# Expert results brought to their tokens by one-hot products instead of indexed stores, in a three-block network on one core

## The chip, the cores and the metric

One core of a Trainium2 chip runs the whole network in one program. The metric is the device time of that program in microseconds (us). Instructions run on TensorE (PE; its weight loads are shown as PEld), VectorE (DVE), ScalarE (ACT), GpSimd (POOL) and SyncE (SP). SP issues most transfers, POOL issues the indexed ones; 16 DMA engines move the data.

## The reference, cut to what matters

Two blocks of attention and dense layers come first and are not touched. The end of the network is a mixture of experts (T = 512 tokens of width 1024, 32 experts with a hidden width of 512, two experts for each token), then a root-mean-square norm:

```python
exp_logits = (t @ w_expert + b_expert)...            # the group is chosen first, then
top_vals, top_idx = lax.top_k(sel_logits, TOP_K)     # TOP_K = 2 experts of it
weights = jax.nn.softmax(top_vals, axis=-1) * g_w
...
hb = jax.nn.silu(xb @ w_gate[e]) * (xb @ w_up[e])    # one expert's rows
ys = hb @ w_down[e]
out = jnp.zeros((n_tok + 1, d), t.dtype).at[row_tok].add(ys * row_w[:, None])
...
x = x + out
return _rms_norm(x, g_final)
```

All is float32. One expert's weights are 6 MiB, all 32 make 192 MiB, and each is read once.

## The kernel before

`moe` runs last. The router's logits give each token its two experts; small matmuls with one-hot matrices then build, for each expert, a list of up to CAP = 64 rows: the token of each row (`li[:, 0]`), the place of its result (`li[:, 1]`, which is 2 * token + choice) and the token's norm factor. The tokens' vectors lie in device memory in `x_d`, written by `router_chunk`.

For each expert e the loop does the following.

- `gather` (L1489, POOL): an indexed transfer brings the expert's rows from `x_d` into `xg` (two buffers).
- `front` (L1495 on): ACT scales the rows (L1497), PE transposes them (L1500) into the PSUM tile `PU`, DVE applies the gain and makes `ex`; then 16 matmuls (L1510) of 64 rows by 512 columns, four for each of four weight slots, gate and up side by side in one PSUM tile (`mm` or `fmm` in turn). ACT takes the silu (L1512), DVE the product `eh`.
- `back` (L1517 on): PE transposes `eh` (L1522), DVE copies it to `ehT` (L1524), 8 matmuls with two weight slots (L1531) fill the PSUM tile `S`, ACT copies it to `ey` (L1534), and POOL stores the 64 rows by an indexed transfer into `y_d` in device memory (L1535).

`front` of expert e stands ahead of `back` of expert e - 1. The weights pass through a ring of `CAPS["ring"]` = 20 slots of 1 MiB (`slot`, L1473 on). SP issues one transfer for each slot (L1485), six for an expert, 192 in all; a slot that is used again waits for the matmuls that read it. The first use of a slot waits for a point in the program before (`gate` in `slot`): slots 0 to 4 the earliest, slots 16 to 19 the finished lists (`ready`). Tiles, waits and the order on each engine come from a scheduling layer.

After the last expert the tokens' vectors are loaded again from `x_d` (L1562), the results from `y_d` (L1607); PE adds one half of each row by matmuls with diagonal matrices of the routing weights (L1609), DVE the other half (L1610); then come squares (L1611, L1612), root, and the scaled result (L1616, L1617), stored by SP (L1618).

Between the loop and this last part stands a branch, `tc.If(most > CAP)` (L1580). Its body repeats experts with more than 64 rows. In the profiled execution the body isn't entered. Each engine loads the count into a register (L1579) and branches; on the way round the body each engine adds to its semaphores what the body would have added, after a wait for all that it has outstanding (the L1580 semaphore instructions of the trace).

Of the kernel before, what the change touches and what calls it, by code (L numbers as in the profile page):

```python
# [18 lines left out]
CAPS = dict(rT=2, m0=6, sb=1, nl=512, g0=5, w=3, wh=2, wl=2, tmp=6, lf=2, kk=2, qq=2, A=2, eu=3, kf=2, xc=2, rq=4, KH=4, KL=4, T=8, Pc=2,  # L19
            P=2, P2=2, pth=3, ptl=3, st=8, stc=2, r4=2, rsx=3, rsy=3, rst=3, hr=2, xtok=2, mh=8, ml=8,  # L20
            hh=22, hl=22, gt=10, sq=2, fw=2, fwh=2, fwl=2, yh=8, yl=8, mgh=8, mgl=8, MKH=4, MKL=4, yt=4, xt=4, ring=20, xgs=2, esg=2, eh=2, ex=2, ehT=2, ey=3, fs=4, fo=4)
# [209 lines left out]
class Net:  # L231
# [1060 lines left out]
    def router_start(self):  # L1292
        self.acc = self.tile([128, 512], F32, name="acc")
        self.pr = self.mmT("tok")
        self.x_d = self.tc.dram_tile([T, D], F32, name="x_d")

    def router_chunk(self, k):
# [8 lines left out]
        if k % 4 == 3:  # L1306

            s = slice(k // 4 * 512, k // 4 * 512 + 512)
            for b in range(4):
# [3 lines left out]
                xt = self.tile([128, 512], F32, name="xt")  # L1313
# [3 lines left out]
    def moe(self, out):  # L1317
        nc, tc = self.nc, self.tc

        list_d = tc.dram_tile([T * NE, 3], I32, name="list_d")  # L1320
        y_d = tc.dram_tile([2 * T, D], F32, name="y_d")
# [124 lines left out]
        place, entry = part(keep, 8, dt=I32), part(keep, 2, 4, 3, dt=I32)  # L1446

        def places():
            exp = part(once, 8)
            nc.gpsimd.tensor_copy(exp[:CAP, :1], last[0][:, :1])  # L1450
            pick(self.c("iota32")[:, None, None, :].to_broadcast(two), exp)
            nc.vector.scalar_tensor_tensor(place, rank, float(NE), exp, op0=OP.mult, op1=OP.add)
            nc.gpsimd.tensor_copy(entry[:, :, :, 0], self.c("tokid")[:, None, :].to_broadcast([128, 2, 4]))
            nc.gpsimd.tensor_copy(entry[:, :, :, 1], row)
            nc.gpsimd.tensor_copy(entry[:, :, :, 2].bitcast(F32), rt[:, None, :].to_broadcast([128, 2, 4]))

        def full_list():
            big = self.tmp()[:, :T * NE * 3 // 128].bitcast(I32)
# [24 lines left out]
        def weights(ap):  # L1483
            w = slot()
            nc.sync.dma_start(w, ap)  # L1485
            return w
# [8 lines left out]
        def front(xg, li_e, wgu, pool="mm"):  # L1495
# [8 lines left out]
            for t in range(4):  # L1504
                w = weights(wgu[t])
# [11 lines left out]
        def back(h, li_e, wd):  # L1517
# [8 lines left out]
            for k in range(4):  # L1526
                if k % 2 == 0:
                    w = weights(wd[k // 2])
# [11 lines left out]
        def wviews(e):  # L1540
            return [self.a[n][e] for n in ("egu", "ed")]

        lists = [[li[:CAP, 0, e:e + 1], li[:CAP, 1, e:e + 1], rtp[:CAP, e:e + 1]] for e in range(NE)]
        gather(xgs[0], lists[0])
        for e in range(NE):
            if e + 1 < NE:
                gather(xgs[(e + 1) % len(xgs)], lists[e + 1])
            w = wviews(e)
            sg = front(xgs[e % len(xgs)], lists[e], w[0], ("mm", "fmm")[e % 2])
            if e:  # L1550
                back(*last)
            last = sg, lists[e], w[1]
            if e == 0:
                places()
        y = back(*last)

        def halves(w):
            return w[:, :D], w[:, D:]
# [4 lines left out]
        dg, gf = halves(slot())  # L1563
        for i in range(8):
            nc.gpsimd.tensor_scalar(dg[:, i * 128:i * 128 + 128], self.c("ident"), s4[:, i // 2, 6 + i % 2:7 + i % 2], None, op0=OP.mult)
        idn = self.tile([128, 128], F32, name="idn")
        self.gate(idn, y)
        nc.gpsimd.tensor_copy(idn, self.c("ident"))
# [11 lines left out]
        with tc.If(most > CAP):  # L1580
            full_list()
            with tc.For_i(CAP * NE, T * NE, CAP * NE) as r0:
                with tc.For_i(0, NE, 1) as e:
                    here = nc.values_load(cnti[0:1, bass.ds(e, 1)], min_val=0, max_val=T)
                    with tc.If(here * NE > r0):
                        li2 = self.tile([CAP, 3], I32, name="li2")
                        lv = list_d[bass.ds(r0 + e, (CAP - 1) * NE + 1), :]
                        src = bass.AP(tensor=lv.tensor, offset=lv.offset, ap=[[NE * 3, CAP], [1, 3]])
                        nc.gpsimd.dma_start(li2, src)
                        lists = [li2[:, 0:1], li2[:, 1:2], li2[:, 2:3].bitcast(F32)]  # L1590
                        gather(xgs[0], lists)
                        w = [self.a[n][bass.ds(e, 1)].rearrange("a k p f -> (a k) p f") for n in ("egu", "ed")]
                        back(front(xgs[0], lists, w[0]), lists, w[1])


        nl = CAPS["nl"]
        lo, hi = slice(0, nl), slice(nl, D)
        pss = [self.mmT(("mm", "fmm", "S", "lev")[b])[:, :nl] for b in range(4)]
        for b in range(4):
            nc.tensor.matmul(pss[b], idn, xt[b][:, lo], start=True, stop=False)  # L1600
        for b in range(4):
            ps, x = pss[b], xt[b]
            yt = self.tile([128, 2, D], F32, name="yt")
            fs = self.tile([128, 4], F32, name="fs")
            o = self.tile([128, D], F32, name="fo")
            y2 = y_d[256 * b:256 * b + 256, :].rearrange("(p j) d -> p j d", j=2)
# [94 lines left out]
```

## Time and profile before

| | us |
|---|---|
| median of 3 runs | 2533.65 (2531.95 to 2535.61) |
| the profiled execution, its own time | 2530.34 |
| its span, first to last instruction | 2528.7 |
| busy in the span: PE / DVE / ACT / POOL | 2378.2 / 1354.2 / 970.2 / 118.5 |

The span is 1.6 us shorter than the execution's own time, and that is 3.3 us under the median. The page counts an engine as busy while an instruction is in it; matmuls overlap in its records (a "mean" of 394 ns doesn't mean one every 394 ns). The expert loop is the last fifth of the span: the first gather starts at 2009 us.

### The profile page before, as it was taken

Reading aid. Unit: us, or ns where it says so; the run is one execution under the profiler, and the core shown is the slowest. Engines: PE = TensorE matmul, PEld = TensorE weight load, DVE = VectorE, ACT = ScalarE, POOL = GpSimd, SP = SyncE. Lnnn points to the kernel's source line nnn. Section 1 sums busy time; section 2 is a strip of 40 time slices with the busy share of each in tenths; the row PEclk is TensorE's granted clock in tenths of the full one; section 3 lists DMA queues with packets and bytes.
Section 4 is the critical chain, followed back from the end, with each engine's and each line's share of the span. In section 5 each row is a group of like instructions: output and inputs, shape, how many; then the busy total and the mean of one; then the engine's idle time right before and its main releaser. Section 6 shows DMA issues by size and latency. Waiting matters only on the chain. (4 is left out here: it accounts for less than half of the span.)

```text
span 2528.7 us, 30232 instructions
## 1 busy us (share of the span) xinstructions
PE 2378.2 (94%) x11330; PEld 1659.3 (66%) x11331; DVE 1354.2 (54%) x3080; ACT 970.2 (38%) x1610; POOL 118.5 (5%) x179
## 2 busy tenths in 40 slices
PE   8999999999999999999999999999999798788775
PEld 6877558888888977558888887777787443222221
DVE  6788876444336878866444338867766411111112
ACT  6544554323225444554232226645444322111111
POOL 0000000000000000000000000000001111111110
PEclk9999999999999999999999999999999899999999
DMA  6133003333334132002333333132234699999997
GB/s 208 36 91 101 18 1 89 94 100 93 100 92 125 36 107 86 9 17 84 94 99 100 92 100 105 51 96 84 78 104 189 232 405 399 406 402 404 409 416 293
DMA packets 83879, 382.08 MB, mean 151 GB/s; under 512 B 12672, under 2 KB 13072, under 8 KB 58512
## 3 DMA queue, kind: packets, MB, share of 16 engines
q1 hardware_dynamic: 77744, 369.60, 41.2%
q0 software_dynamic: 5120, 8.40, 1.0%
q10 hardware_dynamic: 864, 2.10, 0.3%
q8 instruction: 90, 1.47, 0.3%
q14 instruction: 61, 0.50, 0.1%
HBM read 370.61 MB, written 12.59 MB: 152 GB/s over the span
## 5 line engine op out<-in xcount | busy, mean ns | idle before, releaser
L259 ACT ACTIVATE wh<-w 128x1024 fp32r<-128x1024 f32 (+1 forms) x264 | 276.6, 1048 | 624.0 <-PE mm L284 332.7
L283 PE MATMUL mm<-xh,wh 128*128 128x512 f32 x1232 | 489.3, 397 | 9.7 <-ACT wh L259 9.7
L284 PE MATMUL mm<-xl,wh 128*128 128x512 f32 x1232 | 485.4, 394 | 0.0
L285 PE MATMUL mm<-xh,wl 128*128 128x512 f32 x1232 | 484.3, 393 | 0.3 <-DVE wl L260 0.3
L260 DVE TENSOR_TENSOR wl<-w,wh 128x1024 fp32r<-128x1024 f32 (+1 forms) x264 | 321.0, 1216 | 173.1 <-ACT wh L259 172.0
L283 PEld LDWEIGHTS mm<-xh,wh 128*128 128x128 f32 x1232 | 232.5, 189 | 58.8 <-ACT wh L259 9.8
L284 PEld LDWEIGHTS mm<-xl,wh 128*128 128x128 f32 x1232 | 232.3, 189 | 48.7 <-issue 2.9
L285 PEld LDWEIGHTS mm<-xh,wl 128*128 128x128 f32 x1232 | 232.2, 188 | 47.8 <-DVE wl L260 0.9
L253 DVE TENSOR_TENSOR tmp<-mm,xrstd 128x512 f32<-128x512 f32 x104 | 71.7, 690 | 236.5 <-PE mm L285 230.1
L1510 PE MATMUL mm<-ring,ex 128*64 128x512 f32 x512 | 126.2, 628 | 29.5 <-DMA ring<-in_egu_dram 29.1
L1510 PE MATMUL fmm<-ring,ex 128*64 128x512 f32 x512 | 123.3, 615 | 31.5 <-DMA ring<-in_egu_dram 30.7
L283 PE MATMUL mm<-hh,wh 128*128 128x512 f32 x352 | 138.8, 394 | 0.0
L284 PE MATMUL mm<-hl,wh 128*128 128x512 f32 x352 | 138.6, 394 | 0.0
L285 PE MATMUL mm<-hh,wl 128*128 128x512 f32 x352 | 138.1, 392 | 0.0
L1531 PE MATMUL S<-ring,ehT 128*64 128x512 f32 x512 | 124.0, 608 | 11.9 <-DMA ring<-in_ed_dram 10.6
L1510 PEld LDWEIGHTS mm<-ring,ex 128*64 128x64 f32 x512 | 36.2, 142 | 118.6 <-issue 62.6
L1510 PEld LDWEIGHTS fmm<-ring,ex 128*64 128x64 f32 x512 | 35.3, 139 | 116.3 <-issue 59.6
L1497 ACT ACTIVATE xg<-xg,const 64x1024 f32<-64x1024 f32 x32 | 36.6, 1147 | 181.4 <-DMA xg<-x_d,const 181.4
L253 DVE TENSOR_TENSOR eh<-fmm,esg 64x512 f32<-64x512 f32 x16 | 11.1, 693 | 162.9 <-ACT esg L1512 162.9
L550 ACT ACTIVATE P<-S,st,const 128x128 f32<-128x128 f32 (+3 forms) x128 | 78.5, 616 | 50.3 <-DVE st L253 44.4
L253 DVE TENSOR_TENSOR eh<-mm,esg 64x512 f32<-64x512 f32 x16 | 11.1, 693 | 150.0 <-ACT esg L1512 149.9
L623 PE MATMUL O<-pth,nvh 128*64 128x512 f32 (+3 forms) x256 | 89.4, 451 | 1.0 <-DVE pth L593 0.9
(496 smaller groups left out, 4108.1 us busy)
## 6 DMA issues: line engine op xcount, KB each, us to landing
ring<-in_egu_dram SPq DMA_DIRECT2D x128, 1024.0 KB, 21.5
ring<-in_ed_dram SPq DMA_DIRECT2D x64, 1024.0 KB, 21.7
w<-in_fi_dram SPq DMA_DIRECT2D x88, 512.0 KB, 3.6
w<-in_w_dram SPq DMA_DIRECT2D x48, 512.0 KB, 3.7
w<-in_fo_dram SPq DMA_DIRECT2D x44, 512.0 KB, 3.6
w<-in_c_dram SPq DMA_DIRECT2D x16, 512.0 KB, 3.8
tmp<-tmp SPq DMA_DIRECT2D x80, 64.0 KB, 2.0
fw<-in_wo_dram SPq DMA_DIRECT2D x8, 512.0 KB, 3.5
```

Of the source, the lines that this page charges most:

```text
L253: (eng or self.nc.vector).tensor_tensor(out, a, b, op=op)
L259: nc.scalar.activation(hi, src, AF.Copy)
L260: nc.vector.tensor_tensor(lo, src, hi.bitcast(F32), op=OP.subtract)
L283: nc.tensor.matmul(ps, ah, bh, start=first, stop=False)
L284: nc.tensor.matmul(ps, ah, bl, start=False, stop=False)
L285: nc.tensor.matmul(ps, al, bh, start=False, stop=last)
L550: nc.scalar.activation(Ps[q0 + i], S[:, :n], AF.Exp, bias=b, scale=1.0 if scale is None else scale[q0 + i], accum_out=st[:, 1, i:i + 1])
L623: self.nc.tensor.matmul(out, v, p[0], start=first, stop=last)
L1497: nc.scalar.activation(xg[:CAP], xg[:CAP], AF.Copy, scale=li_e[2])
L1510: nc.tensor.matmul(ps[r], x[:, k, :], w[:, at:at + 512], start=k == 0, stop=k == 7)
L1531: nc.tensor.matmul(py[r], hT[:, k, :], w[:, at:at + 512], start=k == 0, stop=k == 3)
```

## The change

The results of two experts are kept in SBUF as a pair of tiles of 128 rows (`eyh`, `eyl`: the routing weight is applied, and the value is split into a float32r part and the rest). For each pair, DVE builds a matrix `esel` (128 rows by 512 tokens) that is 1 where a row belongs to a token (`select`); for each of 4 token blocks and 2 halves of the width PE multiplies it with `eyh` and `eyl` into the PSUM tile `X` (`to_tokens`), and DVE adds `X` to the tokens' vectors, which stay in SBUF (`xt`). `y_d` is gone from the usual path, and so is the second load of `x_d`. `places` prepares what `select` and the weights need (`crow`, `wtp`, `target`). The ring has 18 slots. The branch stands ahead of the last two experts, 30 and 31; their sum to tokens is done after it, straight into the final norm.

```diff
-CAPS = dict(..., nl=512, ..., yt=4, xt=4, ring=20, xgs=2, esg=2, eh=2, ex=2, ehT=2, ey=3, ...)
+CAPS = dict(..., ring=18, xgs=2, esg=1, eh=1, ex=2, ehT=1, eyh=1, eyl=1, esel=1, ...)
...
         def places():
...
+            nc.vector.tensor_scalar(inside, rank, float(CAP), None, op0=OP.is_lt)
+            nc.vector.scalar_tensor_tensor(code, exp, float(CAP), rank, op0=OP.mult, op1=OP.add)
+            nc.vector.scalar_tensor_tensor(code, code, 1.0, inside, op0=OP.add, op1=OP.mult)
...
+            for j in range(2):
+                pb = self.mmT("X")
+                self.spread_pe(pb, code[:, 4 * j:4 * j + 4], 4)
+                nc.scalar.activation(crow[:, j], pb, AF.Copy)
+
+            entw = self.tile([128, 8, 32], F32, name="entw")
+            for j in range(2):
+                self.tt(entw[:, 4 * j:4 * j + 4], ohs[:, 4 * j:4 * j + 4], bc(col(6 + j), 32), OP.mult)
+            pw = self.mmT("X")
+            for r in (slice(0, CAP), slice(CAP, 2 * CAP)):
+                for b in range(8):
+                    nc.tensor.matmul(pw[r, :32], hot[:, b, :], entw[:, b, :], start=b == 0, stop=b == 7)
+            nc.vector.tensor_copy(wtp, pw[:, :32])
...
-            y = self.tile([CAP, D], F32, name="ey")
-            for i, r in enumerate((one, two_)):
-                nc.scalar.activation(y[:, i * 512:i * 512 + 512], py[r], AF.Copy)
-            nc.gpsimd.indirect_dma_start(
-                out=y_d[:, :], out_offset=bass.IndirectOffsetOnAxis(ap=li_e[1], axis=0),
-                in_=y, in_offset=None, bounds_check=2 * T - 1, oob_is_err=False)
-            return y
+            return py
+
+        def weighted(py, e, ys):
+
+            r = (one, two_)[e % 2]
+            for i, s in enumerate((one, two_)):
+                yh, yl = [y[r, i * 512:i * 512 + 512] for y in ys]
+                nc.scalar.activation(yh, py[s], AF.Copy, scale=wtp[s, e:e + 1])
+                nc.vector.scalar_tensor_tensor(yl, py[s], wtp[s, e:e + 1], yh.bitcast(F32), op0=OP.mult, op1=OP.subtract)
+
+        def select(q):
+
+            sel = self.tile([128, T], F32R, name="esel")
+            nc.vector.tensor_scalar(sel, crow[:, 0], target[:, q:q + 1], None, op0=OP.is_equal)
+            nc.vector.scalar_tensor_tensor(sel, crow[:, 1], target[:, q:q + 1], sel.bitcast(F32), op0=OP.is_equal, op1=OP.add)
+            return sel
+
+        def to_tokens(ps, sel, ys, b, s, first=True):
+
+            for i, y in enumerate(ys):
+                nc.tensor.matmul(ps, sel[:, b * 128:b * 128 + 128], y[:, s], start=first and i == 0, stop=i == 1)
...
+        def finish(e, h, wd):
+
+            nonlocal ys
+            if e % 2 == 0:
+                ys = pair()
+            weighted(back(h, wd), e, ys)
+            if e % 2 and e < NE - 1:
+                sel = select(e // 2)
+                for b in range(4):
+                    for s in (lo, hi):
+                        ps = self.mmT("X")
+                        to_tokens(ps, sel, ys, b, s)
+                        self.tt(xt[b][:, s], xt[b][:, s], ps, OP.add)
...
-        for e in range(NE):
-            if e + 1 < NE:
+        for e in range(NE - 2):
+            if e + 1 < NE - 2:
                 gather(xgs[(e + 1) % len(xgs)], lists[e + 1])
...
-        xt = [v for _ in range(2) for v in halves(slot())]
-        for b in range(4):
-            nc.sync.dma_start(xt[b], self.x_d[b * 128:b * 128 + 128, :])
...
+        for e in (NE - 2, NE - 1):
+            wgu[e] = iter(list(wgu[e]))
+            if e == NE - 1:
+                wd[e - 1] = iter(list(wd[e - 1]))
+        wd[e] = iter(list(wd[e]))
...
         with tc.If(most > CAP):
...
-            nc.tensor.matmul(pss[b], idn, xt[b][:, lo], start=True, stop=False)
+            nc.tensor.matmul(pss[b], self.c("ident"), xt[b][:, lo], start=True, stop=False)
+        hs = [up(e) for e in (NE - 2, NE - 1)]
+        sel = select(NE // 2 - 1)
+        for e, h in zip((NE - 2, NE - 1), hs):
+            finish(e, h, wd[e])
+
         for b in range(4):
             ps, x = pss[b], xt[b]
...
-            nc.sync.dma_start(yt, y2)
-            for j in range(2):
-                nc.tensor.matmul(ps, dg[:, (2 * b + j) * 128:(2 * b + j) * 128 + 128], yt[:, j, lo], start=False, stop=j == 1)
-                nc.vector.scalar_tensor_tensor(x[:, hi], yt[:, j, hi], s4[:, b, 6 + j:7 + j], x[:, hi], op0=OP.mult, op1=OP.add)
+            ph = self.mmT("X")
+            to_tokens(ph, sel, ys, b, hi)
+            to_tokens(ps, sel, ys, b, lo, False)
+            self.tt(x[:, hi], x[:, hi], ph, OP.add)
```

Three places show how the order on the engines moves. The first is PE in the loop, from the results of one expert to the first slots of the expert after the next; `ring_...` are weight slots. Before:

```order
L1522 MATMUL PU<-const,eh 128x64 x4
L1500 MATMUL PU<-const,xg_15883 128x64 x8
L1531 MATMUL S<-ring_16631,ehT 64x512 x4
L1531 MATMUL S<-ring_16638,ehT 64x512 x4
L1510 MATMUL fmm<-ring_16667,ex 64x512 x4
L1510 MATMUL fmm<-ring_16674,ex 64x512 x4
```

The same place in the changed kernel:

```order
L1546 MATMUL PU<-const,eh 128x64 x4
L1524 MATMUL PU<-const,xg_15883 128x64 x8
L1555 MATMUL S<-ring_16673,ehT 64x512 x4
L1555 MATMUL S<-ring_16680,ehT 64x512 x4
L1534 MATMUL fmm<-ring_16742,ex 64x512 x3
L1576 MATMUL X<-eyh,esel 128x512
L1534 MATMUL fmm<-ring_16742,ex 64x512
L1534 MATMUL fmm<-ring_16749,ex 64x512
L1576 MATMUL X<-eyl,esel 128x512
L1534 MATMUL fmm<-ring_16749,ex 64x512 x2
L1576 MATMUL X<-eyh,esel 128x512
L1576 MATMUL X<-eyl,esel 128x512
```

The 16 products of a pair of experts now stand among the matmuls of the next `front`, three of which come between the results in `S` and the first product.

The second place is SP's queue where the weights end. Before, the last six weight transfers, the second load of the tokens and the final gain stand ahead of the branch:

```order
L1485 DMA ring_16536<-in_egu_dram 128x2048
L1485 DMA ring_16555<-in_ed_dram 128x2048
L1485 DMA ring_16598<-in_ed_dram 128x2048
L1562 DMA ring_16612<-x_d 128x1024
L1570 DMA ring_16631<-in_g_final_dram 128x1024
L1579 TENSOR_LOAD cmaxi
L1580 COMPARE_AND_BRANCH
```

In the changed kernel, with the branch's two ends and what follows it (the rows of the body, which isn't entered, lie between the two fences):

```order
L1509 DMA ring_16680<-in_ed_dram 128x2048
L1509 DMA ring_16742<-in_ed_dram 128x2048
L1509 DMA ring_16749<-in_ed_dram 128x2048
L1509 DMA ring_16456<-in_egu_dram 128x2048
L1509 DMA ring_16477<-in_egu_dram 128x2048
L1632 TENSOR_LOAD cmaxi
L1633 COMPARE_AND_BRANCH
```

```order
L1633 UNCONDITIONAL_BRANCH x2
L1509 DMA ring_16557<-in_egu_dram 128x2048
L1509 DMA ring_16578<-in_egu_dram 128x2048
L1509 DMA ring_16599<-in_ed_dram 128x2048
L1509 DMA ring_16640<-in_ed_dram 128x2048
L1623 DMA ring_16647<-in_g_final_dram 128x1024
L1694 DMA out_dram<-fo 128x1024 x4
```

Of the 192 weight transfers 184 stand ahead of the branch (the last four of them are expert 30's gate and up), and 8 stand behind it: expert 31's gate and up, and both experts' down weights.

The third place is PE around the branch. Before, two of the four products that bring the tokens into PSUM stand ahead of it and two behind, and no expert's matmul is behind it. In the changed kernel this comes behind it:

```order
L1673 MATMUL tok<-xt_16154,const 128x512
L1524 MATMUL PU<-const,xg_15881 128x64 x8
L1524 MATMUL PU<-const,xg_15883 128x64 x8
L1534 MATMUL mm<-ring_16456,ex 64x512 x4
L1534 MATMUL fmm<-ring_16578,ex 64x512 x4
L1546 MATMUL PU<-const,eh 128x64 x4
L1555 MATMUL S<-ring_16606,ehT 64x512 x4
L1555 MATMUL S<-ring_16640,ehT 64x512 x4
L1576 MATMUL tok<-eyh,esel 128x512 x4
```

All 48 matmuls of experts 30 and 31 stand behind the branch (a row or two of each kind are shown), after four products of the tokens' vectors with the identity.

## Rows read from the trace of the kernel before

**Rows 1.** The page, GB/s moved in 40 equal slices of the span (63 us each).

```profile
GB/s 208 36 91 101 18 1 89 94 100 93 100 92 125 36 107 86 9 17 84 94 99 100 92 100 105 51 96 84 78 104 189 232 405 399 406 402 404 409 416 293
```

**Rows 2.** SP queue's waits, 1900 to 2529 us: total us, times, longest us.

```profile
SPq L1485 <- DMA ring<-in_egu_dram: 249.6, 104, 3.8
```

**Rows 3.** Timeline of POOL: start us, us; first and last gather (15 apart), two stores (3 apart).

```profile
2180.76 0.94 POOL L1489 DMA_INDIRECT xg<-x_d,const  x1 [11.86 <-PE PU L1500]
...
2428.57 0.94 POOL L1489 DMA_INDIRECT xg<-x_d,const  x1 [11.88 <-PE PU L1500]
...
2447.64 0.92 POOL L1535 DMA_INDIRECT y_d<-ey,const  x1 [15.03 <-ACT ey L1534]
...
2492.84 0.89 POOL L1535 DMA_INDIRECT y_d<-ey,const  x1 [14.30 <-ACT ey L1534]
```

**Rows 4.** Two windows: length, busy by engine, PE's granted clock, DMA share, GB/s.

```profile
1936.00:1946.00 10.00, 9.50 (x39) 7.80 (x40) 5.09 (x17) 2.25 (x3) 3.33 (x15) 0.83 1.01 422
...
2505.00:2507.00 2.00, 1.72 (x2) 0.84 (x3) 0.00 (x0) 0.00 (x0) 0.00 (x0) 0.50 0.42 74
```

**Rows 5.** DMA queues, 2433 to 2494 us: POOL's queue: packets, MB, share.

```profile
q0 software_dynamic: 380, 0.55, 2.5%
```

**Rows 6.** Timeline of PE, 2049 to 2125 us, one expert that waits for nothing.

```profile
2049.49 7.06 PE L1510 MATMUL fmm<-ring,ex 128*64 128x512 f32 x32
2056.49 0.46 PE L1522 MATMUL PU<-const,eh 64*128 64x64 f32 x4
...
2057.51 3.65 PE L1531 MATMUL S<-ring,ehT 128*64 128x512 f32 x16
2060.97 7.07 PE L1510 MATMUL mm<-ring,ex 128*64 128x512 f32 x32
```

**Rows 7.** Timeline of PE at 1900 us: two of a run of float32r products.

```profile
1900.22 0.39 PE L283 MATMUL mm<-mgh,wh 128*128 128x512 f32 x1
...
1900.45 0.39 PE L284 MATMUL mm<-mgl,wh 128*128 128x512 f32 x1
```

**Rows 8.** Groups of DVE, 2505 to 2529 us: busy us, mean ns, idle before.

```profile
L1610 DVE SCALAR_TENSOR_TENSOR ring<-yt,const,ring 128x512 f32<-128x512 f32 x8 | 6.0, 751 | 20.3 <-DMA yt<-y_d 20.3
```

**Rows 9.** Timeline of SP at the loop's start: weight transfers issued.

```profile
2011.79 2.15 SPq L1485 DMA_DIRECT2D ring<-in_egu_dram  x4
2020.04 2.19 SPq L1485 DMA_DIRECT2D ring<-in_ed_dram  x2
```

**Rows 10.** DMA issues: KB of one, median us from issue to landing.

```profile
memt<-in_memT_dram SPq DMA_DIRECT2D x1, 1024.0 KB, 4.8
```

**Rows 11.** Timeline of all engines, 2465 to 2529 us.

```profile
2474.17 0.20 PEld L1531 LDWEIGHTS S<-ring,ehT 128*64 128x64 f32 x4 [0.20 <-DMA ring<-in_ed_dram]
...
2494.25 0.20 PEld L1531 LDWEIGHTS S<-ring,ehT 128*64 128x64 f32 x4 [1.31 <-DMA ring<-in_ed_dram]
...
2505.28 2.04 PE L1600 MATMUL mm<-ring,idn 128*128 128x512 f32 x2 [5.73 <-issue]
...
2507.12 1.59 PE L1600 MATMUL S<-ring,idn 128*128 128x512 f32 x2
...
2511.58 0.63 ACT L1612 ACTIVATE fo<-ring 128x512 f32<-128x512 f32 x1 [14.08 <-DVE ring L1610]
...
2512.33 0.60 ACT L1611 ACTIVATE fo<-mm 128x512 f32<-128x512 f32 x1
...
2513.03 1.28 ACT L1614 ACT_TABLE_LOAD   x1
...
2524.07 0.74 DVE L1617 SCALAR_TENSOR_TENSOR fo<-ring,fs,ring 128x512 f32<-128x512 f32 x1
```

**Rows 12.** Chain that ended last: start us, us, what.

```profile
2462.83 41.06 DMA y_d<-ey,const
```

**Rows 13.** Instructions of the branch's line: duration ns, first and last start us.

```profile
L1580 SPq EVENT_SEMAPHORE  x7: 17/17/17, 2488.3 to 2498.7; - x7
...
L1580 POOLq INC_SWDGE_SEM  x1: 1464/1464/1464, 2502.5 to 2502.5; - x1
```

More of the change, by code (lines that the diff above doesn't have):

```diff
@@ L1295, in router_start @@
         self.x_d = self.tc.dram_tile([T, D], F32, name="x_d")
+        self.xt = [self.tile([128, D], F32, name=f"xt{b}") for b in range(4)]
     def router_chunk(self, k):
@@ L1481, in slot, with loads @@
             return ring[i % nring]
[L1483 to L1486, printed above, removed]
+        def loads(ap, n, spare=None):
+            for t in range(n):
+                w = slot() if spare is None else spare[t % len(spare)]
+                nc.sync.dma_start(w, ap[t])
+                yield w
         def gather(xg, li_e):
@@ L1504, in front @@
             for t in range(4):
-                w = weights(wgu[t])
+                w = next(wgu)
                 for kk in range(2):
@@ L1527, in back @@
                 if k % 2 == 0:
-                    w = weights(wd[k // 2])
+                    w = next(wd)
                 for i, r in enumerate((one, two_)):
@@ L1550, in moe @@
             if e:
-                back(*last)
-            last = sg, lists[e], w[1]
+                finish(*last)
+            last = e, h, wd[e]
             if e == 0:
                 places()
-        y = back(*last)
-        def halves(w):
-            return w[:, :D], w[:, D:]
-        xt = [v for _ in range(2) for v in halves(slot())]
-        for b in range(4):
-            nc.sync.dma_start(xt[b], self.x_d[b * 128:b * 128 + 128, :])
-        dg, gf = halves(slot())
-        for i in range(8):
-            nc.gpsimd.tensor_scalar(dg[:, i * 128:i * 128 + 128], self.c("ident"), s4[:, i // 2, 6 + i % 2:7 + i % 2], None, op0=OP.mult)
@@ L1591, in moe @@
-                        gather(xgs[0], lists)
-                        w = [self.a[n][bass.ds(e, 1)].rearrange("a k p f -> (a k) p f") for n in ("egu", "ed")]
[L1593 to L1598, printed above, removed]
-        for b in range(4):
-            nc.tensor.matmul(pss[b], idn, xt[b][:, lo], start=True, stop=False)
+                        src = bass.AP(tensor=lv.tensor, offset=lv.offset, ap=[[NE * 4, CAP], [1, 4]])
@@ new lines, in moe @@
+                        for s in (one, two_):
+                            nc.gpsimd.dma_start(li2[s], src)
+                        li_e = [li2[:CAP, 0:1], li2[:CAP, 1:2], li2[:CAP, 2:3].bitcast(F32)]
+                        gather(xgs[0], li_e)
+                        w = [self.a[n][bass.ds(e, 1)].rearrange("a k p f -> (a k) p f") for n in ("egu", "ed")]
+                        h = front(xgs[0], li_e, loads(w[0], 4, spare))
+                        py = back(h, loads(w[1], 2, spare))
+                        y = self.tile([CAP, D], F32, name="ey")
@@ new lines, in moe @@
+                        for i, s in enumerate((one, two_)):
+                            nc.scalar.activation(y[:, i * 512:i * 512 + 512], py[s], AF.Copy, scale=li2[s, 3:4].bitcast(F32))
+                        nc.gpsimd.indirect_dma_start(
+                            out=y_d[:, :], out_offset=bass.IndirectOffsetOnAxis(ap=li_e[1], axis=0),
+                            in_=y, in_offset=None, bounds_check=2 * T - 1, oob_is_err=False)
+            for b in range(4):
+                y2 = y_d[256 * b:256 * b + 256, :].rearrange("(p j) d -> p j d", j=2)
+                nc.sync.dma_start(yt.rearrange("p (j d) -> p j d", j=2), y2)
+                for j in range(2):
+                    self.tt(xt[b], xt[b], yt[:, j * D:j * D + D], OP.add)
```

60 lines of the change are left out of this document (37 added, 23 removed).

## Prediction

> **What bounds the kernel now.** I read the page's slices first: from the 33rd on, the engines move 399 to 416 GB/s without a gap [rows 1], and the last fifth of the span, the experts, is bound by the weights. The waits of SP say the same: 249.6 us in 104 waits for a weight transfer to land before the next may start [rows 2]. A window in which SP's queue alone runs gives the rate, 422 GB/s [rows 4]; 6 MiB of one expert take 14.9 us at it, one transfer 2.48 us. In the timeline of POOL an expert takes 16.52 us (15 gathers in 247.8 us) where gather and store run, and 15.07 us (three stores in 45.2 us) at the end, where the gathers are over [rows 3]. PE, when it waits for nothing, needs 11.48 us for an expert, from one `front` to the next [rows 6]; it has some 5 us of slack in each. So in the loop only DMA time counts.
>
> The end is different. The last weight arrives at 2494.25 [rows 11], and the chain of waits ends in the indexed stores, which it follows for 41.06 us, one behind the other [rows 12]. After them come the loads from `y_d` and the norm, 34.5 us from the last weight to the end at 2528.7. Between them lies the branch. Its rows show what it is: SP stands from 2488.3 to 2498.7 in semaphore instructions of the branch until its transfers have landed; POOL ends its part at 2502.5 + 1.46 = 2504.0 [rows 13], and PE's first product behind it starts at 2505.28 [rows 11], 1.3 us later. It joins all engines and all transfers.
>
> **The sum.** The landmark is the landing of weight transfer 184, the last one ahead of the branch in the changed kernel. Before, its matmuls are released at 2474.17 [rows 11], and 54.5 us are left.
>
> *Two slots fewer* cost time at the loop's start. Before, slots 16 to 19 are filled by the four transfers at 2011.79; the next transfer needs the first slot back and is issued at 2020.04 [rows 9]. With 18 slots two transfers, 5.0 us of DMA time, fall out of this gap: a transfer takes 4.8 us when it is alone [rows 10], so the engines run dry until about 2023. The engines never idle later, so it isn't won back. The two products `entw` on DVE, ahead of the lists, add some tenths. Together 5.2 us; one transfer (2.5) to three (7.5) are the bounds, three because the small products of `places` also hold up PE's second expert, which frees the next slots. A gain is excluded: nothing is loaded earlier.
>
> *No stores into `y_d`*: 29 of them lie ahead of the landmark. One costs 15.07 - 14.9 = 0.2 us by the periods, and 2.5% of 61 us over four stores = 0.38 us by POOL's share of the engines [rows 5]. I take 0.3: 8.7 us off, bounds 5 and 11. The gathers stay. The second load of `x_d` stands behind the last weight in SP's queue and takes nothing from this landmark.
>
> Transfer 184 then lands at 2474.2 + 5.2 - 8.7 = 2470.7.
>
> *The products of a pair* cost PE 16 x 0.23 = 3.7 us [rows 7], DVE eight additions and two comparisons at 0.75 [rows 8]. A pair then needs 2 x 11.48 + 3.7 = 26.7 us of PE against 32.4 us of DMA: nothing, with 5.8 us of cover for waits between PE and DVE over `X`. `ey` becomes `eyh` on ACT at the same size; `eyl` adds 1.5 us of DVE per expert, off the path.
>
> *The branch* now waits for the additions of experts 28 and 29. Expert 29's down weights land four transfers, 9.9 us, ahead of transfer 184. From there: its matmuls 1.8 (half of 3.65 [rows 6]), `eyh` 0.6, `eyl` twice 1.5, a product 0.5, eight additions 6.0, the last comparisons 1.5, which DVE does ahead of the branch, 11.9 us in all, and 1.3 to release everyone: 13.2 - 9.9 = 3.3 us behind the landmark. Everything behind the branch waits for it, SP's last eight weight transfers too (for SP's own transfers, at least). Bounds: 1.3, when the additions are hidden, and 8, when products and additions alternate instead of overlapping.
>
> *Behind the branch* PE does four products with the identity, of which the trace shows one at 2.04 and a second at 1.59 [rows 11]: with two at full rate (half of 2.04) 5.7 us. Then transposes and `ex` 1.6, two times the 7.0 us of up and gate, two times 1.0 + 3.46 for the transposes and the down product [rows 6]: 30.2 us. The gathers are issued by then. The eight transfers need 4.8 + 7 x 2.48 = 22.2 us from a start at about the landmark, so each lands before PE comes to it: the bound changes from DMA to PE.
>
> [...]
>
> *The norm.* The first result in PSUM 1.9 us after the last down matmul, six squares at 0.75, the table load 1.28, root and reciprocal 0.5, eight scaled products 6.0 and small steps 0.6, then 3.9 us from the last DVE instruction (2524.07 + 0.74) to the end [rows 8, 11]: 18.7 us, bounds 17 and 22. The store and load of `y_d` that stood here are gone.
>
> End: 2470.7 + 3.3 + 30.2 + 18.7 = 2522.9 against 2528.7, 5.8 us less. The profiled execution's own time, 2530.34, becomes 2524.5; the median of the runs is 3.3 us above that execution, so I forecast 2528 us. Most of what the stores give back is lost at the ring, and the two experts behind the branch fill nearly all the time that the loads of `y_d` took.
>
> **Rivals.**
>
> The clock, *slower*: after the branch PE works at the lower level through experts 30 and 31. For: the idle stretch ahead of it is about the one that halves it in [rows 11]. Against: there it recovers within two products, and here PE has work without a gap. Price: 14.0 + 6.9 us of matmuls twice as long, 20.9 us, 2549 us. It decides from 5.8 us of matmul time at half rate on. Chance 0.11.
>
> *No change*: the ring costs its upper bound (7.5) and the additions ahead of the branch overlap only in part (6 instead of 3.3). 5.0 us more, 2533 us. For: both rest on PE waiting for DVE at places which the trace doesn't have. Chance 0.22.
>
> The stores cost what gathers cost, *much faster*: 16.52 - 15.07 = 1.45 us each, 42 us instead of 8.7, 2495 us. For: both move 64 rows of 4 KB by index. Against: 15.07 us with stores is hardly above the bare weights. Chance 0.05.
>
> PE becomes the bound in the loop, *slower*: `X` makes a pair wait over 5.8 us. At 8 us it is 2.2 x 14 = 31 us, 2559 us. Against: PE has matmuls of the next expert between the products. Chance 0.04.
>
> **How the numbers follow.** The forecast has 0.58; its own range, from the bounds added as independent, is 2521 to 2534. With the no-change case inside and half of the clock's case reached, the range is 2518 to 2540. A measurement here can tell 0.2%, 5.1 us, from no change; the forecast lies just beyond, so I give two thirds of its chance to faster, and with the gather case that is 0.45; the rest of it and nearly all of the no-change case make 0.37 for the same; the two slow rivals and the upper edge 0.18.
>
> **What would show it.** The waits of PE for weights stay in the loop, and the period is near 16.2 us. DMA share drops for some microseconds near 2018 and at the branch. Transfer 184 lands near 2471, PE's first product behind the branch starts near 2474, the last down matmul ends near 2504. It is wrong if PE waits for `X` or DVE in the loop, if matmuls behind the branch take about twice 0.43 us, or if the loop's period falls well under 16.

## The result, and the profile after

The changed kernel takes 2628.83 us, the median of four runs (2626.69 to 2633.76), against 2534.63 us (2531.95 to 2538.32) for the kernel before on the same chip: a ratio of 1.0373 (95% interval 1.0361 to 1.0386). It is 94 us slower, where 2528 us were forecast. The profiled execution took 2628.70 us, its span is 2627.1 us, 98.4 us longer than before.

Of its page, the granted clock (tenths of full speed) and the GB/s in 40 slices (66 us each):

```profile
PEclk9999999999999999999999999999998899899998
GB/s 200 42 104 81 9 17 96 97 96 97 97 120 62 62 128 25 1 73 96 96 97 96 97 109 48 93 86 88 104 200 276 355 349 318 318 347 318 321 385 53
```

The expert loop no longer moves 399 to 416 GB/s [rows 1] but 318 to 355 in the 32nd to the 38th slice, and the granted clock falls below 0.9 in two slices of the loop, the 32nd and the 35th. SP's waits (total us, times, longest us) have changed partner too:

```profile
SPq L1509 <- PE fmm L1534: 273.2, 58, 11.8
SPq L1509 <- PE S L1555: 115.9, 55, 5.7
SPq L1509 <- PE mm L1534: 79.0, 56, 7.1
```

Before, SP waited for the transfers ahead of its own [rows 2]; now it waits for PE to give a slot back. DMA has become the one that is kept waiting. Two of POOL's gathers, eight apart, which is four pairs of experts:

```profile
2317.04 0.94 POOL L1513 DMA_INDIRECT xg<-x_d,const  x1 [11.93 <-PE PU L1524]
...
2473.99 0.94 POOL L1513 DMA_INDIRECT xg<-x_d,const  x1 [11.78 <-PE PU L1524]
```

157.0 us for four pairs are 39.2 us a pair; before it was 2 x 16.52 = 33.0 [rows 3].

**Where the 98.4 us lie.** PE's first product of expert 2 and of expert 28, in the kernel before and in the changed one:

```profile
2038.02 3.20 PE L1510 MATMUL mm<-ring,ex 128*64 128x512 f32 x14
...
2430.45 1.94 PE L1510 MATMUL mm<-ring,ex 128*64 128x512 f32 x8 [0.28 <-DMA ring<-in_egu_dram]
```

```profile
2036.64 4.92 PE L1534 MATMUL mm<-ring,ex 128*64 128x512 f32 x22
...
2532.83 2.74 PE L1534 MATMUL mm<-ring,ex 128*64 128x512 f32 x12
```

Up to expert 2 the changed kernel is 1.4 us ahead. From there to expert 28 it takes 496.2 us instead of 392.4: +103.8. From expert 28 to the end it takes 94.3 instead of 98.3: -4.0. The whole loss is in the loop, where the forecast had let PE's added work vanish behind the transfers.

**What happens in a pair.** PE at 2318 us, in the middle of the loop, and ACT in the same stretch (the counts are of trace records: the 512 float32 matmuls of `front`, 512 columns wide, have 1024 of them, the 256 new float32r products 256):

```profile
2318.95 0.50 PE L1576 MATMUL X<-eyh,esel 128*128 128x512 f32 x1 [0.78 <-ACT eyh L1563]
2319.38 1.07 PE L1534 MATMUL fmm<-ring,ex 128*64 128x512 f32 x2
...
2320.81 1.08 PE L1534 MATMUL fmm<-ring,ex 128*64 128x512 f32 x4
2326.45 1.22 PE L1576 MATMUL X<-eyh,esel 128*128 128x512 f32 x2 [4.57 <-ACT eyh L1563]
...
2328.03 1.97 PE L1534 MATMUL fmm<-ring,ex 128*64 128x512 f32 x2
```

```profile
2318.21 0.68 ACT L1563 ACTIVATE eyh<-S,const 64x512 fp32r<-64x512 f32 x1 [3.83 <-PE S L1555]
2324.54 1.15 ACT L1521 ACTIVATE xg<-xg,const 64x1024 f32<-64x1024 f32 x1 [5.65 <-DMA xg<-x_d,const]
2325.72 0.68 ACT L1563 ACTIVATE eyh<-S,const 64x512 fp32r<-64x512 f32 x1
```

`eyh` is made in two halves from the same tile `S`, so both could start at 2318. The second stands behind the scaling of a later expert's rows (L1521), and that waits 5.65 us for a gather which POOL issued at 2317.04. Nothing needs those rows yet: PE transposes them at 2355.69, 31 us later. PE does what matmuls of `front` it has ahead of the product, then stands for 4.57 us. When it goes on, two records of `front` take 1.97 us, where two took 1.07 ahead of the stall. The stall and the 6 us behind it as windows (length; busy us of PE, PEld, DVE, ACT, POOL; granted clock, DMA share, GB/s), and the whole loop:

```profile
2321.00:2326.00 5.00, 0.89 (x4) 0.00 (x1) 0.60 (x1) 1.43 (x2) 0.00 (x0) 0.88 1.02 359
2326.00:2332.00 6.00, 5.55 (x8) 1.70 (x8) 2.13 (x3) 0.40 (x1) 0.00 (x0) 0.53 0.59 218
2036.00:2533.00 497.00, 424.94 (x1786) 150.55 (x1784) 168.78 (x262) 80.16 (x104) 24.32 (x26) 0.93 0.88 337
```

Behind the stall the granted clock is 0.53 over 6 us, where it was 1.00 from 2316 to 2321 us. So one wait is paid twice: once idle, once at nearly half rate (1.97 us for what took 1.07).

The order on ACT late in the loop, before and after the change, shows that the scaling (L1497, now L1521) has moved. It stood behind both halves of `ey`; now it stands between the halves of `eyh`. Why the scheduling layer put it there, the runs don't show:

```
before                                           changed
L1534 ACTIVATE ey<-S 64x512 x2                   L1536 ACTIVATE esg<-mm 64x512
L1497 ACTIVATE xg_15883<-xg_15883,const 64x1024  L1563 ACTIVATE eyh<-S,const 64x512
L1512 ACTIVATE esg<-mm 64x512                    L1521 ACTIVATE xg_15881<-xg_15881,const 64x1024
                                                 L1563 ACTIVATE eyh<-S,const 64x512
                                                 L1536 ACTIVATE esg<-fmm 64x512
```

The wait itself isn't new. ACT's wait for the gathers, in the kernel before over 2036 to 2440 us:

```profile
ACT xg L1497 <- DMA xg<-x_d,const: 155.6, 28, 9.4
```

and in the changed kernel over 2036 to 2533 us, with PE's largest wait there:

```profile
ACT xg L1521 <- DMA xg<-x_d,const: 148.3, 25, 9.1
...
PE X L1576 <- ACT eyh L1563: 59.7, 21, 5.4
```

155.6 us of waiting cost nothing before: both halves of `ey` were out by then, and only a store waited for them. Now one half stands behind that wait, and PE's products wait for it. ACT's rows above show it: the second half of `eyh` started at 2325.72 us, 0.03 us after the end of the scaling, and not at 2318.21, when the first half started from the same tile.

**The end** came out about as counted. PE behind the branch:

```profile
2578.26 6.61 PE L1673 MATMUL tok<-xt,const 128*128 128x512 f32 x8 [3.52 <-DMA xg<-x_d,const]
...
2586.45 7.09 PE L1534 MATMUL mm<-ring,ex 128*64 128x512 f32 x32 [0.43 <-DVE ex L253]
```

The products with the identity take 6.6 us (5.7 forecast), the next matmuls run at full rate, and from 2578.26 to the end of the span it is 48.8 us; 30.2 + 18.7 = 48.9 was forecast.

### The profile page after: what moved, and what is told of

It is laid out like the page before. It is cut to its first block, busy times and chain, and to the rows that moved or that the text cites. A ratio compares the mean times of both kernels' runs of the same rounds, so it can differ in the third digit from the quotient of the medians.

```text
span 2627.1 us, 30810 instructions
## 1 busy us (share of the span) xinstructions
PE 2481.3 (94%) x11606; PEld 1707.6 (65%) x11607; DVE 1496.5 (57%) x3306; ACT 976.4 (37%) x1612; POOL 89.4 (3%) x141
## 3 DMA queue, kind: packets, MB, share of 16 engines
q0 software_dynamic: 2560, 4.20, 0.5%
## 5 line engine op out<-in xcount | busy, mean ns | idle before, releaser
L1534 PE MATMUL fmm<-ring,ex 128*64 128x512 f32 x512 | 168.3, 654 | 0.8 <-DVE ex L253 0.8
L1564 DVE SCALAR_TENSOR_TENSOR eyl<-S,const,eyh 64x512 fp32r<-64x512 f32 x64 | 48.0, 750 | 205.4 <-ACT eyh L1563 205.3
L253 DVE TENSOR_TENSOR xt<-xt,X 128x512 f32<-128x512 f32 x124 | 82.0, 685 | 89.5 <-PE X L1576 89.4
L1555 PE MATMUL S<-ring,ehT 128*64 128x512 f32 x512 | 131.2, 604 | 1.4 <-DVE ehT L1548 1.2
L1576 PE MATMUL X<-eyh,esel 128*128 128x512 f32 x124 | 60.9, 508 | 61.5 <-ACT eyh L1563 61.5
L1534 PE MATMUL mm<-ring,ex 128*64 128x512 f32 x512 | 114.7, 601 | 0.7 <-DVE ex L253 0.7
L1521 ACT ACTIVATE xg<-xg,const 64x1024 f32<-64x1024 f32 x32 | 36.6, 1147 | 192.5 <-DMA xg<-x_d,const 186.8
L1576 PEld LDWEIGHTS X<-eyh,esel 128*128 128x128 f32 x124 | 25.0, 210 | 126.2 <-ACT eyh L1563 81.8
```

The lines of the kernel that those rows point to most:

```text
L253: (eng or self.nc.vector).tensor_tensor(out, a, b, op=op)
L1534: nc.tensor.matmul(ps[r], x[:, k, :], w[:, at:at + 512], start=k == 0, stop=k == 7)
L1555: nc.tensor.matmul(py[r], hT[:, k, :], w[:, at:at + 512], start=k == 0, stop=k == 3)
L1564: nc.vector.scalar_tensor_tensor(yl, py[s], wtp[s, e:e + 1], yh.bitcast(F32), op0=OP.mult, op1=OP.subtract)
L1576: nc.tensor.matmul(ps, sel[:, b * 128:b * 128 + 128], y[:, s], start=first and i == 0, stop=i == 1)
```

## Experiments

The theories, by the letters of the expectations. **S**: the scaling stands ahead of half of `eyh` in ScalarE's queue, and its wait for the gather holds up PE. **L**: ScalarE has too much work or the results come too late, whatever the order. **P**: PE's own work with the products, and its waits for `X`, are the bound. **R**: 18 slots instead of 20 starve the transfers.

**1. The scaling on another engine** (e1_scale_pool). GpSimd issues the gathers and does little else (in the loop of the changed kernel 26 instructions, 24.3 us of 497); behind a scaling only the next gather stands there.

```diff
-            nc.scalar.activation(xg[:CAP], xg[:CAP], AF.Copy, scale=li_e[2])
+            nc.gpsimd.tensor_scalar(xg[:CAP], xg[:CAP], li_e[2], None, op0=OP.mult)
```

> Only the engine that scales the gathered rows is changed (GpSimd in place of ScalarE). Theory S (ScalarE's queue: a half of eyh stands behind the scaling of rows whose gather was issued some 7 us before, TensorE waits for it, and works at the lower clock for a while after): the stall of 8.2 us per pair goes, a pair falls from 39.5 to the 32.4 us of its transfers, and the time to about 2525 us (2515 to 2540). Rival P (the sixteen products and eight additions of a pair themselves, alternating over two X tiles, are the cost): no change beyond 1%, 2605 to 2630. Rival R (the ring of 18 slots starves the transfers): no change either, 2620 to 2630.

Measured 2532.53 us beside 2533.43 of before, ratio 0.9998 (0.9986 to 1.0009). All 96 us are back with one line. The ring, the products and the single buffers of `esg`, `eh` and `ehT` (two each before) are as they were, so P and R fall as the cause of the loss, and so do the buffers. L doesn't fall by this run, since ScalarE has less to do in it. The loop as a window, the columns as above, and PE's wait there:

```profile
2040.00:2432.00 392.00, 384.06 (x1784) 140.97 (x1782) 168.24 (x262) 50.75 (x78) 99.28 (x52) 1.00 1.01 404
```

```profile
PE X L1576 <- ACT eyh L1563: 8.6, 11, 0.8
```

The scaling itself takes longer on GpSimd than the 1.15 us it took on ScalarE, which here costs nothing:

```profile
2299.34 2.84 POOL L1521 TENSOR_SCALAR xg<-xg,const 64x1024 f32<-64x1024 f32 x1 [6.75 <-DMA xg<-x_d,const]
```

The same work (1784 matmul records here, 1786 in the changed kernel) keeps PE busy for 384.1 us here and for 424.9 there, where the clock's mean is 0.93; idle is 7.9 here and 72.1 there. So the loss of 105 us between these windows is 64 us of standing and 41 us of slower work. An estimate from the pair above puts most of the 41 down to the clock: (1 - 0.53) x 6.0 = 2.8 us behind a stall, 37 us in 13 pairs.

**2. No sums in the loop** (e2_no_products). The 16 products and 8 additions of each pair in the loop are left out.

```diff
-                for b in range(4):
-                    for s in (lo, hi):
-                        ps = self.mmT("X")
-                        to_tokens(ps, sel, ys, b, s)
-                        self.tt(xt[b][:, s], xt[b][:, s], ps, OP.add)
```

> Leaves out the products to tokens and the additions of the first 15 pairs (the output lacks these experts' results); eyh, eyl, esel and the place of the scaling in ScalarE's queue stay. S and P both expect the loss to go: the loop runs at its transfers, 2510 to 2530 us. R expects 2600 or more. Between S and P the time of TensorE's up matmuls per expert tells nothing here; what it measures is the price of an indexed store into y_d: the period of an expert late in the loop is 16.2 us if a store costs 0.3 us, 15.1 if it costs as much as a gather.

Measured 2508.38, ratio 0.9903 (0.9883 to 0.9924), just under the 2510 to 2530 that S and P expected. With nobody in the loop waiting for `eyh`, DMA is the bound again (404 GB/s from 2240 to 2280 us), and the price of a store can be read. PE's waits from 2200 to 2420, and two gathers 11 experts apart:

```profile
PE mm L1534 <- DMA ring<-in_egu_dram: 18.8, 25, 2.1
PE fmm L1534 <- DMA ring<-in_egu_dram: 18.3, 26, 2.1
```

```profile
2211.39 0.94 POOL L1513 DMA_INDIRECT xg<-x_d,const  x1 [12.90 <-PE PU L1524]
...
2387.45 0.93 POOL L1513 DMA_INDIRECT xg<-x_d,const  x1 [14.66 <-PE PU L1524]
```

176.1 / 11 = 16.0 us an expert, against 16.52 with the store [rows 3]: a store costs about 0.5 us of DMA time. The single periods in this stretch run from 15.3 to 16.5 us, so the 0.3 that was forecast isn't excluded; the rival in which a store costs what a gather costs, 1.45, falls.

**3. Work to hold the clock** (e3_filler). 20 extra products ahead of the one that waits, whose values are not used.

```diff
+                        if b == 0 and s == hi:
+                            for _ in range(20):
+                                nc.tensor.matmul(ps, sel[:, :128], sel, start=True, stop=True)
```

> Twenty more products of a pair (esel with esel, into an X tile that is overwritten afterwards) are issued on TensorE ahead of the product that waits; nothing else is changed, and the wait on ScalarE stays. S with the clock as part of the loss: the filler (4.6 us at 0.23) lies in the wait, TensorE stays at the higher clock behind it and wins back about 2.8 us in each of 13 pairs: 2592 us (2580 to 2610). S with the wait alone: 2620 to 2635. P (TensorE is simply busy): 4.6 us more per pair, 2680 to 2690.

Measured 2661.05, ratio 1.0497 (1.0479 to 1.0516), which no expectation had. PE around the filler (L1598), and the window:

```profile
2329.68 0.46 PE L1546 MATMUL PU<-const,eh 64*128 64x64 f32 x4 [2.47 <-DVE eh L253]
...
2336.66 4.73 PE L1598 MATMUL X<-esel 128*128 128x512 f32 x17
```

```profile
2330.00:2345.00 15.00, 14.07 (x53) 8.16 (x53) 5.06 (x8) 2.52 (x3) 0.93 (x1) 0.77 0.87 336
```

The filler changed the order, so that in this pair the stall came elsewhere, ahead of it: PE waited for `eh`, and the filler itself met a clock of 0.77 (mean of the window). Over the loop (2036 to 2560 us) PE's waits for `eyh` fall from 59.7 to 32.5 us, those for `eh` rise from 11.1 to 15.8, and the filler adds more than is saved: 17 of its products alone take 4.73 us, some 61 us in 13 pairs. So the run doesn't tell what the clock costs; the windows of experiment 1 do.

**4. Before, with 18 slots** (e4_before_ring18). In the table of the kernel before `ring=20` becomes `ring=18`.

> The kernel before with 18 slots in its ring in place of 20, nothing else. S and the prediction's term: 5.2 us more (2.5 to 7.5), 2539 us. R: 50 us or more above the kernel before.

Measured 2533.51, ratio 0.9998 (0.9987 to 1.0009). SP at the loop's start:

```profile
2008.85 11.32 SPq L1485 DMA_DIRECT2D ring<-in_egu_dram  x4
2021.56 2.04 SPq L1485 DMA_DIRECT2D ring<-in_ed_dram  x2
```

With two slots fewer the first four transfers shown take 11.32 us to issue instead of 2.15, and the next comes at 2021.56 instead of 2020.04 [rows 9]; the time doesn't show it, and R falls a second time. The medians differ by 0.1 us, and the interval allows at most 2.3 us more, so neither the 5.2 us of the prediction nor its lower bound, 2.5, shows in the time. In the profiled execution the stretch from PE's first product of expert 0 to the end is 517.5 us against 512.4, 5.1 more, but the experts began 3.1 us earlier, and one execution of each doesn't decide it.

**5. The scaling on VectorE** (e5_scale_dve). The line of experiment 1 with `nc.vector.tensor_scalar`.

> The changed kernel with the scaling of the gathered rows on VectorE in place of ScalarE. In VectorE's order it then stands between the two halves of eyl, as it stood between the halves of eyh on ScalarE. Theory S (an engine's queue that TensorE's products need waits for a gather): the stall stays, now as a wait for eyl, 2600 to 2645 us. Rival L (ScalarE had too much to do, or is slow at it, and the place in the queue is not the cause): the time falls to that of the kernel with the scaling on GpSimd, 2525 to 2545.

Measured 2587.5, ratio 1.0202 (1.0176 to 1.0227), between the two expectations. DVE at 2300 us:

```profile
2300.00 0.74 DVE L1564 SCALAR_TENSOR_TENSOR eyl<-S,const,eyh 64x512 fp32r<-64x512 f32 x1 [1.57 <-ACT eyh L1563]
...
2305.34 0.74 DVE L1521 TENSOR_SCALAR xg<-xg,const 64x1024 f32<-64x1024 f32 x1 [4.60 <-DMA xg<-x_d,const]
2306.12 0.76 DVE L1564 SCALAR_TENSOR_TENSOR eyl<-S,const,eyh 64x512 fp32r<-64x512 f32 x1
```

ScalarE is relieved, and more than half of the loss stays: the same wait stands in DVE's queue, now ahead of the second half of `eyl`. That speaks against L. The loss is smaller than S had it: PE's waits for `eyl` sum to 34.5 us over the loop (2042 to 2496 us), where those for `eyh` in the changed kernel are 59.7. Why they are shorter was not tested.

**6. Three row buffers** (e6_xgs3): `xgs=3, ring=17`.

> The changed kernel with three buffers for gathered rows in place of two and 17 weight slots in place of 18 (to make room); the scaling stays on ScalarE, and still stands between the two halves of eyh. S: the gather is issued an expert earlier and has landed when ScalarE comes to it, ScalarE waits for no transfer, TensorE doesn't stall: 2528 to 2545 us. Rival L: no change, 2615 to 2640, since ScalarE does the same work.

Measured 2643.84, ratio 1.0426 (1.0403 to 1.045), above both expectations. S had expected the gathers to be early. They were issued an expert earlier, but the scaling moved up with them, and the wait stayed (2036 to 2533 us):

```profile
ACT xg L1521 <- DMA xg<-x_d,const: 158.0, 26, 8.7
```

My expectation missed what the order would be; the run doesn't tell S from L.

**7. The order alone** (e9_order_fix). The scaling stays on ScalarE, at the same length. Two tiny DVE instructions make its factor depend on the last column of `eyh`, times zero, so that both halves of an earlier expert's `eyh` have to stand ahead of it (for the rows of experts 3 to 29).

```diff
+        def hold(e):
+            r = (one, two_)[(e - 2) % 2]
+            z = self.tile([CAP, 2], F32, name="hold")
+            nc.vector.tensor_scalar(z[:, :1], ys[0][r, D - 1:D].bitcast(F32), 0.0, None, op0=OP.mult)
+            nc.vector.tensor_tensor(z[:, 1:2], z[:, :1], lists[e + 1][2], op=OP.add)
+            lists[e + 1][2] = z[:, 1:2]
```

> The changed kernel with the scaling left on ScalarE, two gather buffers and 18 slots; two small VectorE instructions per expert (a multiplication by zero and an addition, 64x1) write the scaling's factor only after both halves of eyh, so that on ScalarE both halves stand ahead of the scaling. Nothing else moves on TensorE. S: the loss goes, as with the scaling on GpSimd: 2532 us (2525 to 2545). L (ScalarE's load or speed is the cause): it does the same work as in the changed kernel, 2615 to 2640.

Measured 2578.21, ratio 1.0169 (1.0152 to 1.0186), about half of the loss back; S had expected 2525 to 2545, L 2615 to 2640. Its loop has two parts:

```profile
2036.00:2125.00 89.00, 88.88 (x414) 33.12 (x412) 40.78 (x72) 18.61 (x24) 5.60 (x6) 1.00 1.01 408
2125.00:2440.00 315.00, 282.53 (x1240) 98.49 (x1236) 124.58 (x221) 57.66 (x75) 16.84 (x18) 0.97 0.99 382
```

The changed kernel in the first 89 us:

```profile
2036.00:2125.00 89.00, 78.35 (x342) 28.22 (x338) 29.11 (x45) 15.17 (x20) 4.67 (x5) 0.92 0.93 356
```

There PE does 414 matmul records instead of 342 without a gap, at full clock, with ACT busier than before (18.61 against 15.17): the order is the cause, not ScalarE's load, and L falls. Later the held scaling comes so late that PE waits for it itself (2100 to 2440 us):

```profile
PE PU L1524 <- ACT xg L1521: 23.3, 8, 2.9
PE X L1576 <- ACT eyh L1563: 7.0, 9, 0.8
```

**8. The branch in the loop** (e7_branch25). With the scaling on GpSimd, the branch ahead of expert 25; all experts run in the loop, the four identity products are dropped, and the last pair goes through `X`.

```diff
-        for e in range(NE - 2):
+        for e in range(NE):
+            if e == 25:
+                finish(*last)
+                last = None
+                overflow()
```

> Scaling on GpSimd, and the branch ahead of expert 25 in place of expert 30; the last pair's sums go through X and VectorE for both halves, so the four products with the identity are gone. If the branch costs because TensorE has two experts' matmuls to do behind it (30 us) while the transfers are over: about 11 us less than with the scaling on GpSimd alone, 2517 us (2510 to 2525). If a branch costs the same wherever it stands: 2528 to 2540.

**9. The branch at the end** (e8_branch_end). The same, with `overflow()` behind all experts and sums.

> As the last, but with the branch behind all experts, where the kernel before has it. Additions of the last pair are over some 31 us after those of the pair before it began, then the branch (2.5 us), then squares, root and scaling: 2524 us (2518 to 2532). If the place ahead of the last two experts is what made the change lose its gain, this one is faster than the one with the scaling on GpSimd alone by 5 us or more; if not, it is equal or slower.

Measured 2527.25, ratio 0.9966 (0.9955 to 0.9978), and 2522.88, ratio 0.9953 (0.9935 to 0.997). The first lies between its two expectations (2510 to 2525, and 2528 to 2540), the second where it was expected. The first products of `front` of experts 24 and 28, with the branch between them (experiment 8) and without it (experiment 1):

```profile
2375.48 2.74 PE L1534 MATMUL mm<-ring,ex 128*64 128x512 f32 x12
...
2443.65 7.04 PE L1534 MATMUL mm<-ring,ex 128*64 128x512 f32 x32
```

```profile
2371.77 7.04 PE L1534 MATMUL mm<-ring,ex 128*64 128x512 f32 x32
...
2432.14 7.04 PE L1534 MATMUL mm<-ring,ex 128*64 128x512 f32 x32
```

That is 68.2 us with the branch and 60.4 without: in the loop it costs PE some 8 us. From expert 24 to expert 25 alone it is 25.6 us against 12.7, but there PE does the down products of expert 24 ahead of the branch instead of behind the next `front`. Behind all experts it costs little (experiment 12), and experiment 9 is 9.7 us faster by the medians than experiment 1, in which the last two experts stand behind the branch.

**10. The best of these** (e10_best): experiment 9, with the first two experts' rows scaled on ScalarE and the last `esel` made before the last results.

> The one with the branch behind all experts, and the first two experts' rows scaled on ScalarE (1.15 us in place of 2.84 each, at the start of the loop where TensorE waits for them); the last comparison ahead of the last additions. 3 us less than with the branch behind all experts: 2520 us (2514 to 2526).

**11. Four PSUM tiles for the pairs' products** (e11_best_lev): `self.mmT("lev")` for `self.mmT("X")`, which has two.

> As e10, with the pairs' products in four PSUM tiles in place of two X tiles. If VectorE's additions, for which TensorE's products wait with two tiles, make a pair take 30.2 us where 26.7 was counted: the loop falls back to its transfers, 2512 us (2506 to 2518). If the products, bunched further ahead, only wait for eyl instead: 2518 to 2535.

**12. No branch at all** (e12_no_branch): experiment 10 without `overflow()`, so that the repeat of overfull experts is left out.

> As e10 without the branch and its body (which this data never enters). The branch then costs what lies between the last addition and the first square, 0.7 us of it needed anyway: 2 us less than e10 (0 to 4). If the join costs more than that row shows: 5 us or more.

Measured 2519.42 (ratio 0.9938, 0.9925 to 0.995), 2516.77 (0.9921, 0.9908 to 0.9934) and 2517.75 (0.9933, 0.992 to 0.9946), beside 2535.26 of before; each lies in its expected range. Without the branch at the end it is 1.7 us less, and the intervals overlap. With four tiles a pair takes 29.1 us (2275 to 2334 us) instead of 30.2; after that it takes 30.5 to 31.6, since PE begins to wait for weights (4.3 us from 2100 to 2460 in the row below), so that its own work and the transfers are nearly level:

```profile
PE mm L1537 <- DMA ring<-in_egu_dram: 4.3, 4, 1.4
```

By the medians experiment 11 is the fastest, 0.8% under the kernel before, with the change's idea kept, its scaling on another engine and its branch moved to the end; the intervals of the three overlap.

## Why the prediction was wrong

**The step that failed** is "*The products of a pair*": "nothing, with 5.8 us of cover for waits between PE and DVE over `X`. `ey` becomes `eyh` on ACT at the same size". The size was nearly right (0.68 us a half, 1.20 for both before). What wasn't read is who waits for it and what stands ahead of it: PE now needs both halves soon after each other, and ACT's queue holds the wait for a gather between them. Half of what was needed stood in the trace of before, 155.6 us of ACT waiting for gathers; the other half stood in the order of ACT's instructions; the prediction looked at the order on PE and SP only. The clock behind a stall was considered behind the branch, not in the loop.

In the sum's own terms, a pair took PE 38.2 us (496.2 / 13) and not 26.7: 3.5 of the difference is there without the stall (30.2 in experiment 1), 4.9 is standing (64 / 13) and 3.1 slower work (41 / 13). Nothing covered the last two, 8.0 us. The cover of 5.8 us was counted against 32.4 us of transfers, but up to expert 28 the kernel before took 392.4 / 13 = 30.2 us a pair, less than its steady 33.0, since PE began with weights already in the ring.

**The rivals.** The nearest is "PE becomes the bound in the loop", with a chance of 0.04 and 2559 us. PE did become the bound, but through ACT and not through `X`. The rival let a pair wait 8 us and took 5.8 of it as covered; that a pair did lose 8.0 us is luck, since neither a queue's wait nor the clock was in it, and none of it was covered. The clock rival, a granted clock as low as the 0.50 of [rows 4] through experts 30 and 31, was placed behind the branch, where PE was back at full clock by the end of the identity products (granted 0.50 from 2578 to 2584 us, 0.95 from 2584 to 2586, 1.00 from 2586 to 2594). The clock fell in the loop (0.53 after 4.57 us idle), which the rival didn't consider, and there the wait was for an engine's queue. The rival that a store costs 1.45 us fell. (It took each list as 64 rows. The 32 gathers of the changed kernel move 4.20 MB in all, 32 rows of 4 KB each on average.)

**The other terms.** The store: 0.3 forecast, about 0.5 measured. The ring: 5.2 forecast, at most 2.3 by the medians. In experiment 2, where the loop goes at the pace of its transfers, SP's last wait at the branch ends at 2457.8, where the landing of transfer 184 was forecast for 2470.7; 5.0 us of that is an earlier start. The unstalled pair on PE: 26.7 forecast, 30.2 in experiment 1 (392 / 13). Where products and `front` alternate there, four of each take 2.14 us:

```profile
2388.05 1.08 PE L1534 MATMUL fmm<-ring,ex 128*64 128x512 f32 x4
...
2390.19 1.08 PE L1534 MATMUL fmm<-ring,ex 128*64 128x512 f32 x4
```

Less four of `front` at 7.06 / 32 [rows 6] that is 0.31 a product instead of 0.23, 1.3 us a pair; the waits for `eyh` are 0.7 a pair (8.6 / 13); the last 1.5 was not settled, but four PSUM tiles instead of two take 1.1 us off the pair (experiment 11). This, too, used up the slack. In experiment 1 SP goes on behind the branch at 2465.70, after transfer 184 has landed (2470.7 forecast; 1.9 us of the difference is an earlier start), but PE's first product behind the branch came at 2476.39, 10.7 later instead of 3.3, and DVE reached the branch only at 2474.9:

```profile
2465.70 2.11 SPq L1509 DMA_DIRECT2D ring<-in_egu_dram  x4
```

```profile
L1633 DVEq COMPARE_BRANCH  x1: 72/72/72, 2474.9 to 2474.9; - x1
```

```profile
2476.39 6.45 PE L1673 MATMUL tok<-xt,const 128*128 128x512 f32 x8 [3.56 <-DMA ring<-in_egu_dram]
```

PE's products and DVE's additions, not the transfers, reached the branch last. Nor does the branch join all engines in experiment 1, as the prediction had read it from the kernel before: SP issued weights behind it 10.7 us ahead of PE's first product there. So even with the queue mended the change gives nothing (0.9998): what the stores give back is spent on PE and at the branch, and experiment 9 gets 9.7 us of it by moving the branch. The part behind the branch held in the changed kernel: 48.9 forecast, 48.8 measured. Its term of 5.7 us takes two of the four identity products at full rate, which no run shows: in the changed kernel the four took 6.6 us, with a granted clock of 0.50 from 2578.26 to 2584 us, and in experiment 1 they took 6.45.

## What to carry to other kernels

When a change makes the engine that sets the pace wait for a result that nobody hurried for before, read the whole queue of the engine that makes it: what stands ahead of each piece, and what that waits for. A wait that costs nothing today (155.6 us here) costs time as soon as something urgent stands behind it (59.7 us of PE's waits for `eyh` here), and moving it to another engine helps only if nobody waits behind it there (on GpSimd all of the loss came back, 2532.5 us against 2628.8, on VectorE less than half, 2587.5). A stall on TensorE is to be priced twice, as idle time and as slower work after it, wherever a trace shows its clock to fall (0.53 over 6 us here).

## What the runs showed of the hardware

- The same scaling of 64 x 1024 float32 takes 1.15 us on ScalarE, 0.74 on VectorE and 2.84 on GpSimd; the slowest gives the fastest kernel here (2532.5 us, against 2587.5 with VectorE and 2628.8 with ScalarE), since only the next gather stands behind it in its queue.
- After 4.57 us of standing, PE's granted clock is 0.53 over the next 6 us, with work at hand (PE busy 5.55 of them); over the loop PE is busy 41 us longer with the same matmuls (424.9 us against 384.1), of which an estimate puts 37 down to the clock.
- A branch that isn't entered costs some 8 us of PE in the middle of the loop (68.2 us for four experts against 60.4); at the end the runs with and without it differ by 1.7 us, which their intervals don't tell apart. In experiment 1 it doesn't join the engines: SP issued weights behind it at 2465.70 us, 10.7 us ahead of PE's first product there.
